# Start of a hybrid decoder step: two column groups in turns, another order of the first transfers, and zero-padded pair matmuls

## The chip, the cores and the metric

The kernel runs on one core of a Trainium2 chip. The metric is the device time of one execution in microseconds (us). Inputs and outputs are float32 and lie in the chip's memory; there is one launch.

## What is computed

One layer of a decoder trunk, for 256 rows of a new sequence (the prompt) and 8 x 4 rows of running sequences (the samples). All 288 rows go through the same weights. Cut to what matters:

```python
proj = x @ w_in                                   # 2048 -> 11280 columns
gB, gC, h, q, k, v, z, b_logit, a_logit, m_a, m_b = split(proj)
conv_out, new_conv_a = causal_depthwise_conv(gC * h, conv_a_buf, conv_a_w)     # width 3
y_a = (gB * conv_out) @ w_a_out
qkv, new_gdn_buf = causal_depthwise_conv(concat(q, k, v), gdn_buf, gdn_conv_w) # width 4
q, k, v = split(silu(qkv)); q, k = l2norm(q), l2norm(k)
o, S = gated_delta_rule(q, k, v, g, beta, S0)     # chunks of 64 rows, 8 heads of 128
y_b = (rms_norm(o) * silu(z)) @ w_b_out
merged = sigmoid(m_a) * y_a + sigmoid(m_b) * y_b
x = layer_norm(ALPHA * x + merged @ w_o)
x = layer_norm(ALPHA * x + relu(x @ w_up)**2 @ w_down)
```

The chunk step of the delta rule is, for each head: `v_new = u - w @ S; o = qd @ S + attn @ v_new; S = S * exp(gl) + kd.T @ v_new`. The convolutions need the last rows of the earlier state (`state_gdn_conv`, `state_conv_a`), here called the history.

## The kernel before, in words

Every large product is cut into **blocks**. A block is a weight tile `raw` of 512 rows (four slices of 128, `KB`) by 256 columns (`GW`), 512 KB. Four blocks that share their 256 columns make a **group** with one accumulator `acc` (two buffers in PSUM); there are 496 blocks. For each block `load` (L164) reads `raw` by a DMA on SyncE's queue, `split_hi` (L173, ScalarE, a cast) and `split_lo` (L179, VectorE, a subtraction) make a rounded high part and the rest, and `matmuls` (L186) issues, for each slice and each half of the columns, three matmuls of 128x128 by 288: hi by xh, hi by xl, lo by xh (L202 to L204). `raw`, `hi` and `lo` have four buffers each. After a group's last block its `evac` functions are called one per following block; they take `acc` out of PSUM and work on. The order of all instructions is written out by hand: the program is one list of blocks, a table `due` of functions to be called ahead of a block, a list `fill` of functions of which one is called behind each triple of matmuls, and generators (`side`) that advance by one step per block.

The activations enter through **`x_tile`** (L732): for each of the 16 slices of 128 features two 128x128 transposes of the prompt and one of the 32 sample rows, on TensorE, then a cast on ScalarE to `xh` and a subtraction on VectorE to `xl`. The columns of x come in four transfers `xr` for the prompt and four of 32 rows for the samples, on SyncE's queue in turns with the first four weight blocks. The 16 transfers of the history (`hwr`, `har`, L723 to L726) are issued on GpSimd's queue from the start on. Eight matmuls on a zero tile (`warm`, L709) come first on TensorE.

The first block's four x tiles come ahead of it; while blocks 0, 1 and 2 run, the twelve others are put between their triples. All three belong to the first group of columns (K, first 256), so block i needs the i-th quarter of x. Weight blocks are split three blocks ahead (`AHEAD`). Constants, layer-norm rows (`lnr`), and the small weight columns `wbar` follow on SyncE's queue (L1286 to L1294). `hist_tiles` (L741) transposes the history and `lnr` at block 4; from there on the convolutions can run. `gates` and then `gdn` (one generator for each half of the heads) are advanced from block 4 on.

In `gdn`, `rep4` (L913) is a copy on GpSimd that lays out the sample keys for a transpose (L917). `aT` holds the masked attention of the 64-row chunks: two heads of a pair lie in partitions 0 to 63 and 64 to 127. For every chunk `p3` (L1188) is the state's update and `p4` (L1192) is `attn @ v_new`, four matmuls with 64 partitions in and 64 out.

Of the kernel before, what the change touches and what calls it, by code (L numbers as in the profile page):

```python
# [9 lines left out]
F32 = mybir.dt.float32  # L10
F32R = mybir.dt.float32r
# [92 lines left out]
def hybrid_kernel(ctx: ExitStack, tc: tile.TileContext, A):  # L104
# [34 lines left out]
    def tt(out, a, b, op):  # L139
        dve.tensor_tensor(out=out, in0=a, in1=b, op=op)  # L140
# [108 lines left out]
    def conv_evac(sec, G, p):  # L249
        def piece(t):  # L250
            hh = 2 * p + t
            ti = sec * 8 + 4 * G + hh
            tl = {}

            def f(ps):
                gpool = gd["pool"]
                w1 = gpool.tile([P, 640], F32, tag="w1", name=nm("w1"), bufs=2)
                pad, cv = w1[:, 0:320], w1[:, 320:640]
                tl["cv"] = cv
                sm = pad[:, 259:315].rearrange("p (b s) -> p b s", s=7)  # L260
                gps.memset(pad[:, 0:3], 0.0)
                gps.tensor_copy(sm[:, :, 0:3], hw[:, ti, 0:24].rearrange("p (b j) -> p b j", j=3))
                act.copy(pad[:, 3:259], ps[:, t, 0:NP_])
                act.copy(sm[:, :, 3:7], ps[:, t, NP_:NT].rearrange("p (b s) -> p b s", s=4))
                c = cv[:, 0:312]
                act.mul(c, pad[:, 0:312], hw[:, ti, 24:25])
                for j in range(1, 4):
                    stt(c, pad[:, j:j + 312], hw[:, ti, 24 + j:25 + j], c, MUL, ADD)
                gps.tensor_copy(stB[:, ti, :].rearrange("p (g j) -> p g j", j=3),
                                pad[:, 256:319].rearrange("p (g s) -> p g s", s=7)[:, :, 0:3])  # L270

            def f2(ps):
# [12 lines left out]
        (a0, a1), (b0, b1) = piece(0), piece(1)  # L285

        def last(ps):
            a1(ps)
            b1(ps)
        return [a0, b0, last]  # L290

    mark = {}
    for G in range(2):
        mark["kqv", G] = len(blocks)
        for sec, c0 in ((1, C_K), (0, C_Q), (2, C_V)):
            for p in range(2):
                add_group(w_in, c0 + 512 * G + GW * p, 0, KT, acts_x, conv_evac(sec, G, p))
        mark["kqv_end", G] = len(blocks)

    def h_evac(p):  # L300
        def f(ps):
# [403 lines left out]
    warm = tx.tile([P, 512], mybir.dt.bfloat16, name="warm")  # L705
    dve.memset(warm, 0.0)
    wps = gtile()
    for _ in range(8):
        pe.matmul(wps, warm[:, 0:P], warm, start=True, stop=True)  # L709
    xr = [tx.tile([P, 3, 512], F32, name=f"xr{i}") for i in range(4)]  # L710
    xpr = A["x_prompt"][0].rearrange("(b p) f -> p b f", p=P)
    xsr = A["x_sample"].rearrange("b t f -> (b t) f")
    sp.dma_start(cf[:, 0:128], A["cf"][:, 0:128])
    for i in range(4):
        c = slice(512 * i, 512 * i + 512)
# [4 lines left out]
    har = tx.tile([76, 256], F32, name="har")  # L720
    for g in range(4):
        c, c2 = slice(768 * g, 768 * g + 768), slice(256 * g, 256 * g + 256)
        gps.dma_start(hwr[28 * g:28 * g + 24, :], A["state_gdn_conv"][0].rearrange("b j c -> (b j) c")[:, c])  # L723
        gps.dma_start(hwr[28 * g + 24:28 * g + 28, :], A["gdn_conv_w"][0][:, c])
        gps.dma_start(har[19 * g:19 * g + 16, :], A["state_conv_a"][0].rearrange("b j c -> (b j) c")[:, c2])
        gps.dma_start(har[19 * g + 16:19 * g + 19, :], A["conv_a_w"][0][:, c2])  # L726
    lnr = tx.tile([33, P], F32, name="lnr")
    gps.memset(epsc[:, 0:1], LN_EPS)
    gps.memset(epsc[:, 1:2], NORM_EPS)
    gps.memset(epsc[:, 2:3], 1.28e-10)  # L730

    def x_tile(k):  # L732
        i, kk = k // 4, k % 4
        g = gtile()
        for b in range(2):
            pe.transpose(g[:, b * P:(b + 1) * P], xr[i][:, b, kk * P:(kk + 1) * P], ident)  # L736
        pe.transpose(g[:, NP_:NT], xr[i][0:NS, 2, kk * P:(kk + 1) * P], ident[0:NS, 0:NS])
        act.copy(xh[:, k, :], g[:, 0:NT])
        tt(xl[:, k, :], g[:, 0:NT], xh[:, k, :], SUB)

    def hist_tiles():  # L741
        g = gtile()
# [114 lines left out]
    def gdn(G):  # L857
# [25 lines left out]
        gps.memset(U128, 0.0)  # L883
        gl = T([P, 4, 2, 64], "gl")
        ss = T([P, 22], "ss")
        red = T([P, 4, 4], "red")
# [23 lines left out]
        pe.transpose(sp2[:, 0:128], kst, ident)  # L910
        pe.transpose(sp2[:, 128:256], qst, ident)

        gps.tensor_copy(wide, four(kst))  # L913
        yield
        ktr = gtile()
        for hh in range(4):
# [246 lines left out]
        for c in range(4):  # L1163
# [24 lines left out]
                pe.matmul(p3[hh % 2][:, hh // 2, :], kdec[r, c, hh // 2, :], v[r, c, hh // 2, :],  # L1188
                          start=True, stop=True)
            for p in range(2):  # L1190
                for par in range(2):
                    pe.matmul(p4[rows[1 - par], p * P:(p + 1) * P], aT[rows[par], 2 * c + p, :], v[rows[par], c, p, :],  # L1192
                              start=True, stop=True)
# [79 lines left out]

    cur = [0]
    aux = []
    his[0] = wp.tile([P, KB, GW], F32R, tag="hi", name=nm("hi"))
    los[0] = wp.tile([P, KB, GW], F32R, tag="lo", name=nm("lo"))
    t = raw.pop(0)
    for k in range(KB + 2):
        if k < KB:  # L1280
            x_tile(k)
        if k > 1:
            act.copy(his[0][:, k - 2], t[:, k - 2])  # L1283
            tt(los[0][:, k - 2], t[:, k - 2], his[0][:, k - 2], SUB)
    load(4)
    sp.dma_start(cf[:, 128:], A["cf"][:, 128:NE])  # L1286
    sp.dma_start(cfe, A["cf"][:, NE:NL])
    sp.dma_start(ci, A["ci"])
    sp.dma_start(lnr[0:16, :], A["ln1_g"].rearrange("o (k p) -> (o k) p", p=P))
    sp.dma_start(lnr[16:32, :], A["ln1_b"].rearrange("o (k p) -> (o k) p", p=P))  # L1290
    sp.dma_start(lnr[32:33, :], A["gdn_norm_w"])
    sp.dma_start(wbar, w_in[:, C_BA:C_BA + 16].rearrange("(k p) c -> p k c", p=P))
    sp.dma_start(arow[:, 0, :], A["a_log"].to_broadcast([P, 8]))
    sp.dma_start(arow[:, 1, :], A["dt_bias"].to_broadcast([P, 8]))  # L1294
    for i in range(3):
        split_hi(i + 1, 2)
        split_lo(i + 1, 2)
        load(i + 5)
        fill.extend(lambda k=k: x_tile(k) for k in range(4 * i + 4, 4 * i + 8))
        matmuls(i)  # L1300
    for i in range(4, AHEAD + 3):
        split_hi(i)
        split_lo(i)
        load(i + 4)
    sgen = side()
    gcm = None
    for p in range(8):
        for n, f in enumerate(residual1(p)):
            at(mark["up"] + 6 + 4 * p + n, f)
    for i in range(3, len(blocks)):  # L1310
        cur[0] = i
        split_hi(i + AHEAD)
        if i == 4:
            hist_tiles()
            tx_cm.__exit__(None, None, None)
            gcm = tc.tile_pool(name="gdn", bufs=1)
# [18 lines left out]
        split_lo(i + AHEAD)  # L1335
        for f in due.pop(i, ()):
            f()
        if i == mark["merge"]:
# [56 lines left out]
```

## Time and profile before

| | us |
|---|---|
| median of 3 runs | 1704.31 |
| lowest and highest | 1704.26, 1704.84 |
| the profiled execution, its own time | 1704.72 |
| its span, first to last instruction | 1702.9 |

The profile is of one execution. Its span leaves out 1.8 us around it; the execution is 0.4 us above the median. In the timeline a row gives start, duration, engine, line, operation, tiles, how many, and in brackets how long the engine sat idle before it and what ended that. PE is TensorE, PEld its weight loads, DVE VectorE, ACT ScalarE, POOL GpSimd, SPq SyncE's DMA queue. Matmuls are pipelined, so the distance of two starts, not the duration, is what one costs.

### The profile page before, as it was taken

The numbers are of one execution on the slowest core, as the hardware profiler recorded it, in microseconds if no ns is written. First come the engines' busy times: TensorE is split into PE (matmuls) and PEld (weight loads), VectorE is DVE, ScalarE is ACT, GpSimd is POOL, SyncE is SP. The second block draws the span as 40 slices with busy tenths as digits, with TensorE's granted clock in tenths as the row PEclk, the third lists the DMA queues.
The fourth block names the chain that finished last, engine by engine and source line by source line (L and its number), as shares of the span: only waits on it lengthen the run. The fifth ranks groups of instructions, "written<-read, shape, count | busy, mean of one in ns | idle before, by whom it ended". The sixth has DMA issues, their size and how long they took to land.

```text
span 1702.9 us, 31111 instructions
## 1 busy us (share of the span) xinstructions
PE 1688.7 (99%) x13077; PEld 1667.2 (98%) x13077; DVE 1013.9 (60%) x1301; ACT 727.6 (43%) x1052; POOL 131.7 (8%) x219
## 2 busy tenths in 40 slices
PE   9999999999999999999999999999999999999997
PEld 7999999999999999999999999999999999999996
DVE  5577885757544444556788744565446554466565
ACT  4675626334543334334445533344334443344331
POOL 2232421023300000000010000000000000000000
PEclk9999999999999999999999999999999999999998
DMA  8464466535655555555565555555555555555552
GB/s 243 141 193 139 122 189 201 149 113 162 183 167 164 171 162 164 170 161 161 166 196 173 168 170 165 162 165 169 162 166 159 170 166 168 162 163 160 173 157 73
DMA packets 272296, 279.69 MB, mean 164 GB/s; under 512 B 12123, under 2 KB 267036, under 8 KB 272024
## 3 DMA queue, kind: packets, MB, share of 16 engines
q1 hardware_dynamic: 267324, 265.80, 51.4%
q0 software_dynamic: 4256, 11.65, 2.5%
q8 instruction: 102, 1.67, 0.4%
q10 hardware_dynamic: 576, 0.26, 0.1%
q14 instruction: 38, 0.30, 0.0%
HBM read 270.19 MB, written 7.48 MB: 163 GB/s over the span
## 4 chain that ended last, share of the span: by engine, by line
PE 99%; DMA 1%; DVE 0%; SPq 0%; issue 0%; ACT 0%
PE acc L202 31%; PE acc L204 31%; PE acc L203 31%; PE g L1021 1%; DMA xr<-in_x_sample_dram 1%; PE g L1009 0%; PE g L1168 0%; PE g L1188 0%; PE g L1192 0%; PE g L1140 0%; PE g L769 0%; PE g L1180 0%; PE g L591 0%; PE g L895 0%; PE g L650 0%; PE g L736 0%
## 5 line engine op out<-in xcount | busy, mean ns | idle before, releaser
L140 DVE TENSOR_TENSOR lo<-raw,hi 128x1024 fp32r<-128x1024 f32 (+2 forms) x502 | 615.7, 1229 | 548.1 <-ACT hi L177 545.5
L177 ACT CAST hi<-raw 128x1024 fp32r<-128x1024 f32 (+1 forms) x498 | 517.8, 1041 | 765.4 <-PE acc L203 711.9
L202 PE MATMUL acc<-xh,hi 128*128 128x288 f32 x1408 | 422.3, 300 | 0.2 <-ACT hi L1283 0.2
L204 PE MATMUL acc<-xh,lo 128*128 128x288 f32 x1408 | 416.4, 296 | 0.0
L203 PE MATMUL acc<-xl,hi 128*128 128x288 f32 x1408 | 416.2, 296 | 0.0
L202 PE MATMUL acc<-dh,hi 128*128 128x290 f32 x1024 | 303.9, 297 | 0.0
L203 PE MATMUL acc<-dl,hi 128*128 128x290 f32 x1024 | 303.2, 296 | 0.0
L204 PE MATMUL acc<-dh,lo 128*128 128x290 f32 x1024 | 302.7, 296 | 0.0
L204 PE MATMUL acc<-hh,lo 128*128 128x288 f32 x1024 | 302.3, 295 | 0.0
L203 PE MATMUL acc<-hl,hi 128*128 128x288 f32 x1024 | 302.3, 295 | 0.0
L202 PE MATMUL acc<-hh,hi 128*128 128x288 f32 x1024 | 302.2, 295 | 0.0
L202 PEld LDWEIGHTS acc<-xh,hi 128*128 128x128 f32 x1408 | 265.2, 188 | 2.8 <-issue 0.7
L203 PEld LDWEIGHTS acc<-xl,hi 128*128 128x128 f32 x1408 | 265.5, 189 | 0.9
L204 PEld LDWEIGHTS acc<-xh,lo 128*128 128x128 f32 x1408 | 265.3, 188 | 0.0
L202 PEld LDWEIGHTS acc<-dh,hi 128*128 128x128 f32 x1024 | 193.6, 189 | 0.1
L204 PEld LDWEIGHTS acc<-dh,lo 128*128 128x128 f32 x1024 | 193.3, 189 | 0.0
L203 PEld LDWEIGHTS acc<-dl,hi 128*128 128x128 f32 x1024 | 193.3, 189 | 0.1
L203 PEld LDWEIGHTS acc<-hl,hi 128*128 128x128 f32 x1024 | 192.5, 188 | 0.0
L204 PEld LDWEIGHTS acc<-hh,lo 128*128 128x128 f32 x1024 | 192.3, 188 | 0.0
L202 PEld LDWEIGHTS acc<-hh,hi 128*128 128x128 f32 x1024 | 192.1, 188 | 0.0
L203 PE MATMUL acc<-ml,hi 128*128 128x288 f32 x256 | 75.6, 295 | 0.0
L204 PE MATMUL acc<-mh,lo 128*128 128x288 f32 x256 | 75.6, 295 | 0.0
(389 smaller groups left out, 1614.3 us busy)
## 6 DMA issues: line engine op xcount, KB each, us to landing
raw<-in_w_in_dram SPq DMA_DIRECT2D x176, 512.0 KB, 3.6
raw<-in_w_up_dram SPq DMA_DIRECT2D x128, 512.0 KB, 3.7
raw<-in_w_down_dram SPq DMA_DIRECT2D x128, 512.0 KB, 3.7
raw<-in_w_o_dram SPq DMA_DIRECT2D x32, 512.0 KB, 3.7
raw<-in_w_a_out_dram SPq DMA_DIRECT2D x16, 512.0 KB, 3.6
raw<-in_w_b_out_dram SPq DMA_DIRECT2D x16, 512.0 KB, 3.6
S<-in_state_gdn_dram POOLq DMA_DIRECT2D x8, 512.0 KB, 7.7
out_dram<-S POOLq DMA_DIRECT2D x8, 512.0 KB, 4.9
```

Of the source, the lines that this page charges most:

```text
L140: dve.tensor_tensor(out=out, in0=a, in1=b, op=op)
L177: act.copy(his[i][:, k:k + step], raw[i][:, k:k + step])
L202: pe.matmul(o, wh, xh_, start=st, stop=False)
L203: pe.matmul(o, wh, xl_, start=False, stop=False)
L204: pe.matmul(o, wl, xh_, start=False, stop=en)
L1021: pe.matmul(out[r, q * 64:q * 64 + 64], a[r, q, :], b[r, q, :], start=True, stop=True)
```

## The change

Five things are changed.

1. The first eight blocks, two groups, are taken in turns: slices 0 to 3 of the first group, slices 0 to 3 of the second, then 4 to 7 of each, and so on. Blocks 2u and 2u+1 need the u-th quarter of x. Both accumulators are in use until block 7. The first group's conv functions for its two halves are called together (`pair`).
2. All sample rows come by one transfer (`xs4`, 128 partitions) on ScalarE's queue and are transposed by four full transposes (`x_sample`). The prompt is transposed four tiles at a time (`x_steps`), and cast and subtracted two slices at a time. The first quarter of the prompt comes in two halves, one on ScalarE's queue. Eleven warm matmuls stand first and four more behind the sample's transposes. The second half of `fill` in blocks 1, 3 and 5 holds the later quarters.
3. The weight splits of the first blocks run two blocks ahead and are issued behind the matmuls of a block. SyncE's queue now has two weight blocks, a quarter of x, two weight blocks, a quarter of x; the constants come one by one behind blocks 2 to 5.
4. The history's 16 transfers wait until `xr[2]` has landed (a one-element copy on GpSimd), and the three of `lnr` follow them on the same queue. `hist_tiles` stands ahead of block 6, `gates` from block 10.
5. In `gdn`, `aT` is 128 wide with zeros, cleared on GpSimd, so that `p4` is two matmuls of 128 by 128 for a chunk; `rep4` is filled by ScalarE.

```diff
+        def pair(ps):
+            a0(ps)
+            b0(ps)
+        if G == 0 and sec == 1 and p == 0:
+            return [pair, last]
...
+    blocks[0:8] = [blocks[4 * (u % 2) + u // 2] for u in range(8)]
...
-    for _ in range(8):
-        pe.matmul(wps, warm[:, 0:P], warm, start=True, stop=True)
-    xr = [tx.tile([P, 3, 512], F32, name=f"xr{i}") for i in range(4)]
+    warm_up(11)
+    xr = [tx.tile([P, 2, 512], F32, name=f"xr{i}") for i in range(4)]
+    xs4 = tx.tile([P, 512], F32, name="xs4")
...
-        sp.dma_start(xr[i][:, 0:2, :], xpr[:, :, c])
-        sp.dma_start(xr[i][0:NS, 2, :], xsr[:, c])
-        load(i)
+    act.dma_start(xr[0][:, :, 256:512], xpr[:, :, 256:512])
+    act.dma_start(xs4, xsr)
+    sp.dma_start(cf[:, 0:128], A["cf"][:, 0:128])
+    sp.dma_start(xr[0][:, :, 0:256], xpr[:, :, 0:256])
+    load(0)
+    load(1)
+    sp.dma_start(xr[1], xpr[:, :, 512:1024])
+    load(2)
+    load(3)
+    sp.dma_start(xr[2], xpr[:, :, 1024:1536])
...
+    gps.tensor_copy(hwr[0:1, 0:1], xr[2][0:1, 0, 0:1])
     for g in range(4):
...
+    gps.dma_start(lnr[0:16, :], A["ln1_g"].rearrange("o (k p) -> (o k) p", p=P))
+    gps.dma_start(lnr[16:32, :], A["ln1_b"].rearrange("o (k p) -> (o k) p", p=P))
+    gps.dma_start(lnr[32:33, :], A["gdn_norm_w"])
...
+    def x_sample():
         g = gtile()
+        for c in range(4):
+            pe.transpose(g[:, c * P:(c + 1) * P], xs4[:, c * P:(c + 1) * P], ident)
...
+        act.copy(xv, gv)
+        tt(xw, gv, xv, SUB)
+
+    def x_steps(i):
+        def prompt(u):
...
+            def turn(k, b):
+                c = (2 * u + k) * P
+                return lambda: pe.transpose(gv[:, k, b * P:(b + 1) * P], xr[i][:, b, c:c + P], ident)
+
+            def out():
+                ks = slice(4 * i + 2 * u, 4 * i + 2 * u + 2)
+                act.copy(xh[:, ks, 0:NP_], gv)
+                tt(xl[:, ks, 0:NP_], gv, xh[:, ks, 0:NP_], SUB)
...
-        aT = T([P, 8, 64], "aT")
+        aT = T([P, 8, P], "aT")
         gps.memset(kqm, 0.0)
-        gps.memset(U128, 0.0)
+        for z in (U128, aT):
+            gps.memset(z, 0.0)
...
-        gps.tensor_copy(wide, four(kst))
+        act.copy(wide, four(kst))
...
-            tt(aT[rows[par]],
+            tt(aT[rows[par], :, 64 - 64 * par:128 - 64 * par],
...
-                for par in range(2):
-                    pe.matmul(p4[rows[1 - par], p * P:(p + 1) * P], aT[rows[par], 2 * c + p, :], v[rows[par], c, p, :],
-                              start=True, stop=True)
+                pe.matmul(p4[:, p * P:(p + 1) * P], aT[:, 2 * c + p, :], v[:, c, p, :], start=True, stop=True)
...
+    for f in x_steps(0):
+        f()
+    x_sample()
+    warm_up(4)
+    split_hi(0, 1)
+    split_lo(0, 1)
...
+    split_hi(1, 2)
+    split_lo(1, 2)
     load(4)
...
+    load(5)
+    sp.dma_start(xr[3], xpr[:, :, 1536:2048])
...
-    for i in range(3, len(blocks)):
+    for i in range(len(blocks)):
         cur[0] = i
-        split_hi(i + AHEAD)
-        if i == 4:
+        if i == 6:
+            split_hi(i + 2)
+            split_lo(i + 2)
+        if i > 5:
+            split_hi(i + AHEAD)
+        if i in (1, 3, 5):
+            a_, b_ = x_steps(i // 2 + 1)
+            idle = lambda: None
+            fill.extend([idle, idle, idle, a_, idle, b_])
+        if i == 6:
             hist_tiles()
...
-        if i > 3 and sgen:
+        if i > 9 and sgen:
...
         matmuls(i)
-        load(i + AHEAD + 4)
+        if i < 6:
+            split_hi(i + 2)
+            split_lo(i + 2)
+            load(i + 6)
+        if i == 6:
+            load(i + 6)
+        if i > 5:
+            load(i + AHEAD + 4)
+        if 2 <= i < 6:
+            rest[i - 2]()
```

More of the change, by code (lines that the diff above doesn't have):

```diff
@@ L707, in hybrid_kernel, with warm_up @@
     wps = gtile()
-    for _ in range(8):
-        pe.matmul(wps, warm[:, 0:P], warm, start=True, stop=True)
-    xr = [tx.tile([P, 3, 512], F32, name=f"xr{i}") for i in range(4)]
-    xpr = A["x_prompt"][0].rearrange("(b p) f -> p b f", p=P)
[L712 to L715, printed above, removed]
-        sp.dma_start(xr[i][:, 0:2, :], xpr[:, :, c])
-        sp.dma_start(xr[i][0:NS, 2, :], xsr[:, c])
-        load(i)
+    def warm_up(n):
+        for _ in range(n):
+            pe.matmul(wps, warm[:, 0:P], warm, start=True, stop=True)
+    warm_up(11)
+    xr = [tx.tile([P, 2, 512], F32, name=f"xr{i}") for i in range(4)]
+    xs4 = tx.tile([P, 512], F32, name="xs4")
+    xpr = A["x_prompt"][0].rearrange("(b p) f -> p b f", p=P)
+    xsr = A["x_sample"].rearrange("b t (j f) -> j (b t) f", j=4)
     hwr = tx.tile([112, 768], F32, name="hwr")
     har = tx.tile([76, 256], F32, name="har")
+    lnr = tx.tile([33, P], F32, name="lnr")
+    act.dma_start(xr[0][:, :, 256:512], xpr[:, :, 256:512])
[8 more added lines that the diff above has]
+    sp.dma_start(xr[2], xpr[:, :, 1024:1536])
+    gps.memset(epsc[:, 0:1], LN_EPS)
+    gps.memset(epsc[:, 1:2], NORM_EPS)
+    gps.memset(epsc[:, 2:3], 1.28e-10)
+    gps.tensor_copy(hwr[0:1, 0:1], xr[2][0:1, 0, 0:1])
     for g in range(4):
@@ L726, in hybrid_kernel, with step, f @@
         gps.dma_start(har[19 * g + 16:19 * g + 19, :], A["conv_a_w"][0][:, c2])
[L727 to L733, printed above, removed]
-        g = gtile()
[L735 to L739, printed above, removed]
+    gps.dma_start(lnr[0:16, :], A["ln1_g"].rearrange("o (k p) -> (o k) p", p=P))
+    gps.dma_start(lnr[16:32, :], A["ln1_b"].rearrange("o (k p) -> (o k) p", p=P))
+    gps.dma_start(lnr[32:33, :], A["gdn_norm_w"])
+    def x_sample():
+        g = gtile()
+        for c in range(4):
+            pe.transpose(g[:, c * P:(c + 1) * P], xs4[:, c * P:(c + 1) * P], ident)
+        gv = g.rearrange("p (c j t) -> p j c t", c=4, j=4)
+        xv, xw = (u.rearrange("p (j c) t -> p j c t", j=4)[:, :, :, NP_:NT] for u in (xh, xl))
+        act.copy(xv, gv)
+        tt(xw, gv, xv, SUB)
+    def x_steps(i):
+        def prompt(u):
+            g = gtile()
+            gv = g.rearrange("p (k t) -> p k t", k=2)
+            steps = []
+            def turn(k, b):
[5 more added lines that the diff above has]
+                tt(xl[:, ks, 0:NP_], gv, xh[:, ks, 0:NP_], SUB)
+            return [turn(k, b) for k in range(2) for b in range(2)], out
+        def step(part):
+            def f():
+                turns, out = part()
+                for g in turns:
+                    g()
+                out()
+            return f
+        return [step(lambda: prompt(0)), step(lambda: prompt(1))]
     def hist_tiles():
@@ L1275, in hybrid_kernel @@
     aux = []
[L1276 to L1284, printed above, removed]
-    load(4)
[L1286 to L1304, printed above, removed]
+    for f in x_steps(0):
[4 more added lines that the diff above has]
+    split_lo(0, 1)
+    rest = [lambda: sp.dma_start(cf[:, 128:], A["cf"][:, 128:NE]),
+            lambda: sp.dma_start(cfe, A["cf"][:, NE:NL]),
+            lambda: sp.dma_start(wbar, w_in[:, C_BA:C_BA + 16].rearrange("(k p) c -> p k c", p=P)),
+            lambda: (sp.dma_start(ci, A["ci"]),
+                     sp.dma_start(arow[:, 0, :], A["a_log"].to_broadcast([P, 8])),
+                     sp.dma_start(arow[:, 1, :], A["dt_bias"].to_broadcast([P, 8])))]
+    split_hi(1, 2)
+    split_lo(1, 2)
+    load(4)
+    load(5)
+    sp.dma_start(xr[3], xpr[:, :, 1536:2048])
     sgen = side()
@@ L1334, in hybrid_kernel @@
                 gd["ao"] = ap_.tile([P, 2, H, NT], F32, tag="ao", name="ao")
-        split_lo(i + AHEAD)
+        if i > 5:
+            split_lo(i + AHEAD)
         for f in due.pop(i, ()):
@@ L1360, in hybrid_kernel @@
         matmuls(i)
-        load(i + AHEAD + 4)
+        if i < 6:
[4 more added lines that the diff above has]
+            load(i + 6)
+        if i > 5:
+            load(i + AHEAD + 4)
+        if 2 <= i < 6:
+            rest[i - 2]()
     for i in sorted(due):
```

## The prediction, made before the changed kernel was run

> **What bounds the kernel now.** I read the page first (busy times, then the chain that ended last), then the start of TensorE's timeline, where most of the change lies, then the queues that feed it.
>
> ```profile
> span 1702.9 us, 31111 instructions
> PE 1688.7 (99%) x13077; PEld 1667.2 (98%) x13077; DVE 1013.9 (60%) x1301; ACT 727.6 (43%) x1052; POOL 131.7 (8%) x219
> PE 99%; DMA 1%; DVE 0%; SPq 0%; issue 0%; ACT 0%
> ```
>
> TensorE is the bound from end to end: a gain needs work taken off TensorE, or its slow start shortened. Busy is not busy at full speed, so the start's rows come next.
>
> ```profile
> 1.19 3.60 PE L709 MATMUL g<-warm 128*128 128x512 bf16 x8 [1.19 <-DVE warm L706]
> 9.57 0.61 PE L202 MATMUL acc<-xh,hi 128*128 128x288 f32 x1 [0.21 <-ACT hi L1283]
> 18.35 0.44 PE L202 MATMUL acc<-xh,hi 128*128 128x288 f32 x1
> 18.59 0.44 PE L203 MATMUL acc<-xl,hi 128*128 128x288 f32 x1
> 23.27 0.30 PE L203 MATMUL acc<-xl,hi 128*128 128x288 f32 x1
> 23.40 0.29 PE L204 MATMUL acc<-xh,lo 128*128 128x288 f32 x1
> 24.26 0.30 PE L203 MATMUL acc<-xl,hi 128*128 128x288 f32 x1
> 31.25 0.30 PE L202 MATMUL acc<-xh,hi 128*128 128x288 f32 x1
> 34.44 0.55 PE L744 MATMUL g<-cf,hwr 112*128 112x112 f32 x4
> 35.43 0.40 PE L202 MATMUL acc<-xh,hi 128*128 128x288 f32 x1
> ```
>
> Product matmuls start 0.24 apart at 18.35 and 0.13 apart at 23.27: at 18.35 TensorE still runs at about half speed, and the eight warm matmuls had not cured it. Block 3 starts at 31.25 and takes 34.44 - 31.25 = 3.19; the history's transposes take 35.43 - 34.44 = 0.99. An x tile stands between the matmuls of 23.40 and 24.26; without it they would be 2 x 0.13 apart, so it costs 0.60. At 31.25, then, three blocks (9.6) and 16 x tiles (9.6) are done, and 12 us went to waiting and half speed.
>
> **Part 1: the start.** Four full transposes in the tail show the price of a batch of the new kind, and two views show how fast data arrives:
>
> ```profile
> 1612.07 0.30 PE L204 MATMUL acc<-hh,lo 128*128 128x288 f32 x1
> 1612.20 0.60 PE L591 MATMUL g<-cf,acc 128*128 128x128 f32 x4
> 1612.56 0.38 PE L202 MATMUL acc<-hh,hi 128*128 128x288 f32 x1
> 1612.77 0.29 PE L203 MATMUL acc<-hl,hi 128*128 128x288 f32 x1
> ```
>
> ```profile
> 0.00:10.00 10.00, 7.50 (x22) 3.33 (x22) 2.09 (x6) 3.37 (x7) 6.46 (x16) 1.00 0.78 212
> 10.00:20.00 10.00, 9.15 (x35) 7.15 (x35) 5.27 (x12) 4.41 (x11) 2.19 (x7) 1.00 1.09 299
> ```
>
> ```profile
> 9.12 0.40 ACT L1283 CAST hi<-raw 128x256 fp32r<-128x256 f32 x1 [0.17 <-DMA raw<-in_w_in_dram]
> 18.27 1.14 ACT L177 CAST hi<-raw 128x512 fp32r<-128x512 f32 x2 [0.30 <-DMA raw<-in_w_in_dram]
> ```
>
> The batch costs (1612.77 - 1612.07) - 0.26 = 0.44. The last two columns of the windows are the DMA engines' share and GB/s. The bytes moved are 2.12 MB by 10 us and 0.30 MB per us after that; the queues are full (share 1.09). Block 0's weights had landed at 9.12, when about 1.9 MB had moved, and block 2's at 18.27, after 4.6 MB; counting all that was issued ahead of them (constants, x, weights, history), 1.4 and 3.8 MB. So a transfer lands when its own running sum plus 0.5 to 0.8 MB has moved. The new order's sums (x quarter, weight block: 0.52 MB each, samples 0.26, first constants 0.07) are 1.4 MB for block 0's weights, 1.9, 2.4 for the second x quarter, 2.9 for block 2, 3.5, and 4.0 for the third quarter. Their landings come out at 9.0, 11, 13, 14.7, 16.5 and 18.3.
>
> The first product matmul thus starts where it does now: I take 9.7, since ScalarE must cast a sample batch first. From there block 0 needs 3.2 plus 0.3 for its first low part (13.2). Block 1 needs 3.2 and two batches, 4.1 in all (17.3). Block 2's weights land at 14.7, and cast, subtraction and one x subtraction follow: 1.05, 1.23 (below) and an estimated 0.65 by width give 17.6. Blocks 2 to 5 take 3.2 + 4.1 + 3.2 + 4.1, up to 32.2, with every transfer there at least 2 us early. Then six blocks and all of x are done, against three at 31.25: 3 x 3.19 - 0.95 = **8.6 gained**. Later rows stay as they are, since TensorE has no idle time there that the order of groups could change.
>
> This assumes full speed from 9.7. Eleven warm matmuls last 11 x 0.45 = 5 us from 1.19, and four more stand behind the samples. If the speed comes only at 12.8, 3.1 us at half cost 1.5, of which 0.4 hides in block 2's wait: 1.1. The rule that bears on it is in the Trainium skill, "TensorE: Matmul & The Clock Gate", Part 1: full clock follows one busy window of 3.4 us that runs freely, and Part 4 adds that transposes hardly count as busy. By that rule the new warm-up holds a whole window in about 4 of 10 phases, and the sum would lose up to 1.1 in the others. The trace agrees in that 3.60 us of warm matmuls left half speed behind; no row fixes the phase.
>
> **Part 2: the history's wait.** It is moved behind the third x quarter and three transfers longer, and TensorE, which works in order, meets it at block 6. Queued behind it there are all blocks from 6 on.
>
> ```profile
> 1.29 0.70 POOL L723 DMA_DIRECT2D hwr<-in_state_gdn_conv_dram  x1 [0.84 <-POOLq L1382]
> 6.27 0.52 POOL L723 DMA_DIRECT2D hwr<-in_state_gdn_conv_dram  x1 [0.75 <-DMA hwr<-in_state_gdn_conv_dram]
> 12.48 0.51 POOL L726 DMA_DIRECT2D har<-in_conv_a_w_dram  x1
> ```
>
> ```profile
> DMA to landing us min/median/max: 4.5/6.4/7.2
> ```
>
> ```profile
> DMA to landing us min/median/max: 1.8/3.2/4.7
> ```
>
> The first landing row is that of `hwr` at the start, with full queues; the second is that of the state's output (L1262), later. Eight transfers go out 0.51 apart, and the ninth waits for the first one's landing (6.27). So 19 transfers are two such rounds and three more: with landings of L, the last one lands 3L + 1.5 after the first issue, or 9.7 + L where L is under 4.1. Now sixteen are issued in 11.7 us; three more and a landing make it 19.5. At the short end it is 9.7 + 3.2 = 12.9. From 18.3 the history is there at 31.2 to 37.8. The weight queue is full early in that stretch and emptier at its end, so I take the middle, 34.6: TensorE waits **2.4** at 32.2. Bounds: nothing to 5.6.
>
> A long wait can also cost speed:
>
> ```profile
> 1680.00:1686.00 6.00, 5.45 (x42) 5.22 (x40) 0.96 (x4) 0.00 (x0) 0.00 (x0) 1.00 0.00 0
> 1686.00:1690.00 4.00, 1.44 (x7) 0.61 (x7) 3.77 (x14) 0.68 (x3) 0.00 (x0) 0.85 0.00 0
> 1690.00:1694.00 4.00, 3.30 (x9) 1.90 (x8) 3.78 (x12) 0.52 (x2) 0.00 (x0) 0.50 0.42 157
> ```
>
> The granted clock (third column from the end) falls to half some 3 us after the last dense matmuls. Getting it back took from about 12.4 to 19.7 at the start, 3.6 us lost; with dense matmuls I take 2.5. It applies to waits above 3.4 only.
>
> **Part 3: the chunks.**
>
> ```profile
> 192.69 0.65 PE L1192 MATMUL g<-v,aT 64*64 64x128 f32 x8
> 193.28 0.49 PE L1102 MATMUL g<-b 128*128 128x128 f32 x2
> 193.52 0.38 PE L202 MATMUL acc<-xh,hi 128*128 128x288 f32 x1
> 205.18 0.60 PE L1180 MATMUL g<-v,U 128*128 128x128 f32 x4
> 205.62 0.39 PE L1120 MATMUL g<-b 128*128 128x128 f32 x2
> 205.76 0.38 PE L202 MATMUL acc<-xh,hi 128*128 128x288 f32 x1
> ```
>
> The quarter-size matmuls take 193.28 - 192.69 = 0.59 per chunk; two full ones (L1180) take 0.44. Behind the small tiles the next pair takes 0.24, behind full ones 0.14: up to 0.10 for the switch, which may only move to p3. So 0.15 to 0.25 for each of 8 chunks, 1.2 to 2.0; I take **1.6**. A rule speaks against it: the Trainium skill, "TensorE: Matmul & The Clock Gate", Part 3, has small tiles in different rows and columns run together, and then the pairs would cost what the full ones do, and the sum would be 1.6 smaller. The trace disagrees by half: 0.074 apiece against 0.11 for full ones, not 0.055.
>
> **Edits at nothing.** The moved copy and the larger clear have cover:
>
> ```profile
> L913 POOL COPY vmh<-kqs x2: 942/1012/1081, 102.0 to 286.0; 128x512 f32<-128x512 f32 x2
> L883 POOL MEMSET U<- x2: 955/974/993, 90.2 to 265.2; 128x1024 f32 x2
> ACT hi L177 <- PE acc L203: 155.5, 79, 4.4
> L177 ACT CAST hi<-raw 128x1024 fp32r<-128x1024 f32 (+1 forms) x498 | 517.8, 1041 | 765.4 <-PE acc L203 711.9
> L140 DVE TENSOR_TENSOR lo<-raw,hi 128x1024 fp32r<-128x1024 f32 (+2 forms) x502 | 615.7, 1229 | 548.1 <-ACT hi L177 545.5
> ```
>
> ScalarE waits 79 times between 60 and 500 us for a free buffer of hi, so 0.6 more there is hidden; without that cover it costs 1.2 in all. The second clear adds 1 us to GpSimd, which is 8% busy. At block 7 the first group's evacuation must free its accumulator within 3.19: one cast (1.05) and some 1.7 of copies and scaling fit, if block 10's weights are there. With both accumulators held, a late one costs up to 1; I take nothing. The gates start six blocks later but end one block later.
>
> **The sum.** 8.6 - 2.4 + 1.6 = 7.8 off the profiled execution's 1704.7, hence off the median of 1704.3 too: **1696.5**.
>
> **Rivals.**
> - History in time: nothing waits at block 6, 10.2 gained: 1694.1; with a start half a microsecond earlier and the upper chunk price 1693. For it: fewer weights are in flight by then. Against: full queues at 18 us. 0.17.
> - History late by 5.6 with the clock lost: 10.2 - 5.6 - 2.5 = 2.1, 1702.2. For it: the first landing row. 0.18.
> - Slower: the same wait, at block 6. It eats the whole gain when it passes 7.7 us, that is when landings average 6.7; at 7.8 the result is 3.4 slower, 1707.7. Against: the longest landing shown is 7.2. 0.05.
> - The warm-up doesn't do what it says, or the chunks give nothing: 1697.6 and 1698.1. 0.10.
>
> **How the numbers follow.** The forecast has 0.50. About 0.2% (3.4 us) can be told from no change, so faster means under 1700.9. The forecast, the first and the last rival lie there, and a small part of the second with a shorter wait: 0.82. Same takes most of the second, 0.12; slower is 0.06. The range runs from 1693 to 1702, which takes in both bounds of the wait.
>
> **What would show it.** Right: 0.13 spacing from the first product matmuls on, block 6 near 32, an idle row of 1 to 4 us at the history's transposes with a GpSimd transfer as its releaser, p4 in four passes of 0.11. Wrong: idle time between blocks 1 to 5 (weights later than my sums), 0.24 spacing beyond 13 us, a wait for the accumulator at block 8, or an idle row at the history above 6 us.

## The result, and the profile after

The changed kernel is slower: 1710.11 us (median of 6 runs, 1709.41 to 1711.23) against 1704.57 of the kernel before beside it, a ratio of 1.0034 with a 95% interval of 1.0024 to 1.0044. The forecast of 1696.5 was wrong in its sign. The profiled execution took 1709.7 us. Its page, with the busy times and the chain that ended last:

```profile
span 1707.8 us, 31019 instructions
PE 1684.7 (99%) x13040; PEld 1667.2 (98%) x13040; DVE 1012.4 (59%) x1292; ACT 727.0 (43%) x1045; POOL 123.5 (7%) x223
PE 90%; DVE 2%; ACT 1%; issue 1%; POOL 0%; ACTq 0%; DVEq 0%
```

The share of TensorE is 99% as before, but it is idle for 1707.8 - 1684.7 = 23.1 us, against 14.2 before, and the chain now runs through VectorE and ScalarE for some per cent. TensorE's waits name two places that the kernel before does not have (total, times, longest, in us):

```profile
PE g L965 <- ACT vmh L961: 6.0, 1, 6.0
PE g L757 <- DMA xs<-in_x_sample_dram: 3.8, 1, 3.8
```

The start, and the place of the long wait, in TensorE's timeline:

```profile
11.26 1.11 PE L757 MATMUL g<-cf,xs 128*128 128x128 f32 x4 [3.77 <-DMA xs<-in_x_sample_dram]
13.52 0.80 PE L202 MATMUL acc<-xh,hi 128*128 128x288 f32 x1
16.76 0.44 PE L202 MATMUL acc<-xh,hi 128*128 128x288 f32 x1
17.41 0.29 PE L202 MATMUL acc<-xh,hi 128*128 128x288 f32 x1
37.16 0.55 PE L791 MATMUL g<-cf,hwr 112*128 112x112 f32 x4
38.14 0.40 PE L202 MATMUL acc<-xh,hi 128*128 128x288 f32 x1
110.02 1.12 PE L965 MATMUL g<-cf,vmh 128*128 128x128 f32 x4 [6.01 <-ACT vmh L961]
110.79 0.59 PE L202 MATMUL acc<-xh,hi 128*128 128x288 f32 x1
115.00 0.29 PE L202 MATMUL acc<-xh,hi 128*128 128x288 f32 x1
```

The first product matmul comes at 13.52 (9.57 before), because the samples land late, and half speed (durations of 0.44 and more) lasts to about 17.2. The warm matmuls had brought full speed: the granted clock is 0.91 over 8 to 11 us; the 3.77 us of waiting for the samples lost it again (0.50 from 11 to 17.2). The history's transposes at 37.16 show no wait. Block 6 starts at 38.14, in the kernel before at 41.91:

```profile
41.91 0.29 PE L202 MATMUL acc<-xh,hi 128*128 128x288 f32 x1
```

So the start did gain, 3.8 us. At 104.0 TensorE then stands for 6.01 us ahead of the transposes of `rep4`. These take 110.79 - 110.02 = 0.77 instead of 0.36 (rows of the kernel before, below), and block 24 behind them 115.00 - 110.79 = 4.21 instead of 3.19, both at half speed at first.

What the wait is for is read from the two engines behind it. ScalarE, then GpSimd, both of the changed kernel:

```profile
90.07 1.28 ACT L866 ACT_TABLE_LOAD   x1
95.04 0.56 ACT L266 ACTIVATE w<-w,hw 128x312 f32<-128x312 f32 x1 [1.89 <-POOL w L262]
101.76 0.56 ACT L266 ACTIVATE w<-w,hw 128x312 f32<-128x312 f32 x1 [2.37 <-POOL w L262]
105.63 1.28 ACT L276 ACT_TABLE_LOAD   x1
109.35 0.62 ACT L961 COPY vmh<-kqs 128x512 f32<-128x512 f32 x1
```

```profile
92.05 0.22 POOL L879 COPY gpt<-qt 64x48 f32<-64x48 f32 x1 [7.60 <-ACT qt L870]
95.09 3.59 POOL L911 DMA_DIRECT2D S<-in_state_gdn_dram  x4
98.67 1.08 POOL L929 MEMSET b<- 128x1152 f32 x1
99.67 0.98 POOL L931 MEMSET U<- 128x1024 f32 x1
100.57 0.97 POOL L931 MEMSET aT<- 128x1024 f32 x1
101.50 0.22 POOL L262 COPY w<-hw 128x24 f32<-128x24 f32 x1
```

The copy `rep4` (L961) comes at 109.35, at the end of a queue on ScalarE that was held up twice by GpSimd, at the convolution's evacuation (L266 needs GpSimd's L262). GpSimd in turn was busy first with the gate copies (`gpt`, `gsw`), which had themselves waited 7.60 for ScalarE, then with the set-up of `gdn`: the state's four loads and three clears, 95.09 to 101.5. In the kernel before the same set-up lay where nobody waited, and the copy was early:

```profile
85.62 3.60 POOL L864 DMA_DIRECT2D S<-in_state_gdn_dram  x4
90.20 0.99 POOL L883 MEMSET U<- 128x1024 f32 x1
101.97 0.94 POOL L913 COPY vmh<-kqs 128x512 f32<-128x512 f32 x1
104.33 0.60 PE L917 MATMUL g<-cf,vmh 128*128 128x128 f32 x4
104.69 0.38 PE L202 MATMUL acc<-xh,hi 128*128 128x288 f32 x1
```

So by block 111 of 496 the changed kernel is 4.6 behind: +3.8 from the start and +1.1 from the chunks (priced below), -6.0 for the wait, -1.4 for the half speed behind it (0.4 at the transposes, 1.0 in block 24), -0.9 for four short waits at blocks 47 to 94 that the kernel before does not have either. That is -3.4; the other 1.2 is spread over rows that I have not named.

### The profile page after: what moved, and what is told of

Same layout as the page of the kernel before. It is cut to its first block, busy times and chain, and to the rows that moved or that the text cites. A ratio compares the mean times of both kernels' runs of the same rounds, so it can differ in the third digit from the quotient of the medians.

```text
span 1707.8 us, 31019 instructions
## 1 busy us (share of the span) xinstructions
PE 1684.7 (99%) x13040; PEld 1667.2 (98%) x13040; DVE 1012.4 (59%) x1292; ACT 727.0 (43%) x1045; POOL 123.5 (7%) x223
## 4 chain that ended last, share of the span: by engine, by line
PE 90%; DVE 2%; ACT 1%; issue 1%; POOL 0%; ACTq 0%; DVEq 0%
PE acc L202 29%; PE acc L203 29%; PE acc L204 29%; PE g L1069 1%; DVE lo L140 1%; DVE w L143 1%; PE g L1057 0%; PE g L1236 0%; PE g L1239 0%; PE g L1188 0%; PE g L1216 0%; PE g L598 0%; PE g L657 0%; DVE v L143 0%; ACT hi L177 0%
## 5 line engine op out<-in xcount | busy, mean ns | idle before, releaser
L140 DVE TENSOR_TENSOR lo<-raw,hi 128x1024 fp32r<-128x1024 f32 (+1 forms) x500 | 613.2, 1230 | 541.6 <-ACT hi L177 539.4
```

## The experiments

Three candidates stood for the 6 us: the copy's place on ScalarE (A), the later gates and all that hangs on them (B), the extra clear (C). A fourth theory (D) concerned the samples' landing.

**The copy on GpSimd again.**

```diff
-        act.copy(wide, four(kst))
+        gps.tensor_copy(wide, four(kst))
```

> The changed kernel with one edit undone: the copy rep4 is on GpSimd again. In the changed kernel (1710.1) TensorE waits 6.01 us for this copy at 104.0, and runs some 3 us at half speed behind it, about 7.4 us in all. Theory A (the copy's place on ScalarE costs it, since it stands there behind late casts): GpSimd is idle from 101.9 on, so the copy is done by about 103, TensorE does not wait, and the time is 1702.5 to 1704. Theory B (ScalarE as a whole is late, because GpSimd's gate copies, state loads and clears come six blocks later and hold up the convolutions' evacuation): the wait moves to the next thing that comes from ScalarE, at least 3 us of it stay, 1706 or more.

Measured: 1708.47, ratio 1.0018 (1.0008 to 1.0027). B's forecast is met, A's is not. TensorE's wait:

```profile
PE g L965 <- POOL vmh L961: 3.4, 1, 3.4
```

and the copy in GpSimd's timeline:

```profile
108.33 1.54 POOL L961 COPY vmh<-kqs 128x512 f32<-128x512 f32 x1 [3.92 <-DVE red L948]
```

The wait is 2.6 shorter, so A explains less than half of it. I had overlooked a reader: `rep4` shares its buffer with the squares that VectorE reduces (L948), and these come from ScalarE, so the copy is late on any engine when ScalarE is late. This profile had a wait of 1.6 at block 6 besides, for `lnr`, so the profiled execution gained almost nothing.

**The gates from block 7.**

```diff
-        if i > 9 and sgen:
+        if i > 6 and sgen:
```

> The changed kernel with the gates started at block 7 rather than 10; the copy rep4 stays on ScalarE, the clear of aT on GpSimd. Theory B: GpSimd's four pairs of gate copies come near 82 rather than at 92, so the state loads (3.59) and the clears (3.0) lie ahead of the evacuation that ScalarE begins at 98.9, ScalarE's two waits for GpSimd (1.89 and 2.37) go, the copy comes some 4 to 5 us earlier, TensorE waits under 1.5 us, and the time is 1703 to 1705. Theory A: the copy still stands behind ScalarE's casts, the wait stays at 4 us or more, and the time is 1708 or more.

Measured: 1700.91, ratio 0.9979 (0.997 to 0.9989), 9.2 below the changed kernel, and faster than before. B is confirmed, with 2 us more than its 1703 to 1705. Of ScalarE's two waits for GpSimd the one of 2.37 is gone; one of 1.89 stays behind the gate copies, but it now ends at 84.3 and not at 95.0, far ahead of the copy `rep4`. The set-up now runs 84.36 to 90.7, ahead of the evacuation of 92.4, and the copy still on ScalarE costs TensorE little:

```profile
84.36 3.59 POOL L911 DMA_DIRECT2D S<-in_state_gdn_dram  x4
100.46 0.66 PE L965 MATMUL g<-cf,vmh 128*128 128x128 f32 x4 [0.69 <-ACT vmh L961]
```

**The chunks as they were.** `aT` 64 wide, not cleared, `p4` in eight small matmuls.

> The changed kernel with the chunk outputs p4 as they were: aT 64 wide, no clear of it, eight quarter-size matmuls per chunk. Theory C (the clear of aT, 0.97 us on GpSimd ahead of the evacuation's copy, makes the wait): the wait falls by as much as the clear took, to 5.0 us, or goes altogether if a turn of the queue hangs on it; the chunks cost 8 x 0.2 = 1.6 more; 1710.7, or 1704.5 if it goes. Theory A and B: the wait stays between 5 and 6 us, and the difference to the changed kernel is the price of the chunks less one microsecond: 1710 to 1711. If the padded pairs gain nothing, 1709.

Measured: 1709.65, ratio 1.0031 (1.0019 to 1.0043). The wait is 5.1 instead of 6.0: the clear is worth about what it lasts (0.97) and no more. C falls as the main cause. The time is 0.4 below what A and B gave (1710 to 1711), which the interval (3.2 to 7.3 us above the kernel before) can't tell from it.

**The samples on SyncE's queue.**

```diff
-    act.dma_start(xs4, xsr)
     sp.dma_start(xr[0][:, :, 0:256], xpr[:, :, 0:256])
+    sp.dma_start(xs4, xsr)
```

> The changed kernel with the one DMA of the samples moved from ScalarE's queue to SyncE's, behind the first quarter of x and ahead of block 0's weights. In the changed kernel the samples are there at 11.26 only, though issued at 1.25, and the first product matmul starts at 13.52. Theory D (ScalarE's queue gets a small share of the transfers beside SyncE's full one, and that is what makes the start late): the samples land after 0.85 MB, at 6 to 7 us, the first product matmul starts at 9.7 to 10.5, and 3 to 3.8 us are gained: 1706.3 to 1707.1. Rival (the transfers as a whole are the limit, whatever their queue): the weights of block 0 come 0.26 MB later, the first product matmul at 11.5 or later, and the time is 1708 to 1710. If half speed then lasts as long after the first product matmul as now (3.7 us), the gain is the same; if it ends at the same time (17.2), half of it goes.

Measured: 1709.36, ratio 1.0029 (1.0019 to 1.0039). D is right on the start and wrong on the total:

```profile
8.65 0.66 PE L757 MATMUL g<-cf,xs 128*128 128x128 f32 x4 [1.70 <-DMA xs<-in_x_sample_dram]
10.35 0.40 PE L202 MATMUL acc<-xh,hi 128*128 128x288 f32 x1 [0.17 <-ACT hi L177]
35.99 0.22 PE L796 MATMUL g<-cf,lnr 33*128 33x33 f32 x1 [2.48 <-DMA lnr<-in_gdn_norm_w_dram]
```

```profile
38.00:40.00 2.00, 2.00 (x10) 2.00 (x10) 0.00 (x0) 0.00 (x0) 0.00 (x0) 0.50 0.87 184
```

Block 0 starts 3.2 earlier and at full speed, block 5, for that, 4.5 earlier. At block 6 stands the wait that the prediction had put there, 2.48 long (forecast 2.4). By its row it is for `lnr`, whose three transfers the change put behind the history's on the same queue; the history's own transposes, just ahead of it, show no wait. Behind it the granted clock is 0.50 (in the row of the windows, third column from the end) and block 6 takes 4.82 instead of 3.29. So 4.0 of the 4.5 are given back at once.

**The later gates alone, in the kernel before** (`i > 3` becomes `i > 9`).

> The kernel before with one edit of the change alone: the gates start at block 10 instead of 4. Everything else, the start and the copy on GpSimd too, stays as before (1704.6). Theory B (the later gates alone push GpSimd's gate copies, state loads and clears onto the evacuation, and ScalarE with them): TensorE waits 2.4 to 3.4 us at the transposes of rep4 (3.36 in the run with the copy on GpSimd, less up to one for the clear that is not there) and loses 1 to 1.5 behind it: 1708 to 1709.5. Rival E (the later gates hurt only together with the faster start, which leaves ScalarE and GpSimd less time up to there): the wait is under 1 us, 1704 to 1705.5.

Measured: 1709.37, ratio 1.0029 (1.0018 to 1.004). This one edit makes the kernel before as slow as the whole change did. The waits of TensorE and of ScalarE:

```profile
PE g L917 <- POOL vmh L913: 2.5, 1, 2.5
ACT w L266 <- POOL w L262: 3.4, 2, 1.9
```

B again; rival E, that it needs the faster start, falls.

**Padded pairs alone, and the copy on ScalarE alone, in the kernel before.**

> The kernel before with the zero-padded pairs alone (aT 128 wide and cleared as a whole, p4 in four passes). In the run with the gates from block 7 each of the 8 chunks came out 0.15 us shorter against the kernel before. If that is the edit's price: 1.2 less than before, 1703.3 (the prediction's 1.6 would give 1702.9; pairs that cost what the small tiles do, 1704.5). If the clear of aT ahead of the evacuation's copy made a wait there of its own, as theory C had it, TensorE would show a wait of about 1 us at the transposes of rep4 and the time would be 1704.5.

> The kernel before with the copy rep4 on ScalarE alone, the gates where they were. The prediction held it hidden in ScalarE's waits (nothing lost, 1704.5). Theory A in what is left of it: it stands behind a cast and four small copies there, as in the run with the gates from block 7, and TensorE waits 0.3 to 0.8 us for it at the first group's transposes: 1704.8 to 1705.3.

Measured: 1703.10 with the pairs, ratio 0.9991 (0.9982 to 1.0), and 1704.43 with the copy, ratio 0.9998 (0.9989 to 1.0007). A chunk in the first:

```profile
192.44 0.71 PE L1192 MATMUL g<-v,aT 128*128 128x128 f32 x4
192.99 0.39 PE L1103 MATMUL g<-b 128*128 128x128 f32 x2
193.13 0.38 PE L202 MATMUL acc<-xh,hi 128*128 128x288 f32 x1
```

The four passes take 0.55 (the small ones 0.59), the pair behind them 0.14 (0.24): 0.14 per chunk, and each chunk brings the blocks behind it forward by that much, 1.1 for all eight. The medians differ by 1.6, with an interval of 0 to 3.1. In the second, TensorE does not wait at `rep4` at all. Where the gates come early, both edits are as harmless as the prediction had them.

**Where in the queues the later gates hurt.** Six runs separate the parts. First the eight gate copies (`gpt`, `gsw`) moved from GpSimd to VectorE:

> The changed kernel with the gates as late as there, and their eight copies (gpt, gsw) on VectorE instead of GpSimd. In the changed kernel GpSimd stands idle for 7.60 us until 92.05 for these copies' operand, with the state loads (3.59) and the clears (3.0) queued behind them, and ScalarE's evacuations then wait 1.89 and 2.37 for GpSimd. Theory G (it is GpSimd's order that does it): the loads and clears are done by 91, ScalarE's two waits go, the copy rep4 comes 4.3 us earlier, TensorE waits 1.7 us or less at its transposes and keeps its clock or loses up to 1: 1702.5 to 1705. Rival S (ScalarE is late of itself, by its table loads of 1.28 us for the gates and back between 85 and 107): the wait stays at 3 us or more, 1706.5 or more.

Measured: 1710.56, ratio 1.0036 (1.0022 to 1.005), a wait of 6.3, which is what rival S gave (3 us or more, 1706.5 or more). Theory G falls as I had put it: GpSimd still met the evacuation's last copy, which waits for ScalarE, and did the set-up from 94.87 to 101.2, ahead of the next evacuation; ScalarE waited 3.3 for it in one piece.

Then the first group's steps moved against the evacuations. These come one per block behind a group, at blocks 20 and 21, then 24 and 25. The set-up stands between those of 20 and 21 in the changed kernel, ahead of both with the gates from block 9 (`i > 8`), behind both in the other run (`mark["kqv", G] + 20` becomes `+ 22` for the first half of the heads):

> The changed kernel with the gates from block 9 instead of 10, so that the first group's set-up (state loads, clears) stands one block earlier, at block 20 as in the kernel before. Theory H (the set-up's 6.6 us on GpSimd must lie in the long pause between two groups' evacuations; it hurts where it stands ahead of an evacuation that ScalarE already wants): behind the gate copies it would start near 89 and end near 96, and the evacuation of about 92 waits for it some 4 us, so most of the loss stays: 1707 to 1711. Rival L (each block of lateness costs, wherever it lies): a third of the way to the run with block 7, 1706 to 1707, with a wait of 3 to 4 us.

> The changed kernel with the gates as late as there, and the first group's set-up two blocks later still (from block 22 on), behind both evacuations of the group that ends at block 19. Theory H: GpSimd's 6.6 us then lie between 97 and 104, ahead of the next group's evacuation at about 107; ScalarE's wait of 2.37 goes and the copy rep4 comes early enough: TensorE waits under 1.5 us, 1702 to 1704.5, though the set-up is later. Rival L: later is worse, TensorE waits 6 us or more, 1710 or more.

Measured: 1709.36, ratio 1.0029 (1.0018 to 1.0039), with a wait of 6.4; and 1708.61, ratio 1.0023 (1.0014 to 1.0033), with a wait of 1.7 there. ScalarE's longest wait for GpSimd in the first, and TensorE's at a chunk in the second:

```profile
ACT w L266 <- POOL w L262: 4.8, 1, 4.8
```

```profile
PE g L1236 <- DVE v L140: 2.0, 1, 2.0
```

One block earlier doesn't help, since the set-up then holds up the evacuation ahead of which it stands, for 4.8. Behind the evacuations it holds up nobody, and the wait falls to 1.7 (H: under 1.5). But the time missed its forecast by 4: the steps that are now two blocks late wait later, 2.0, 1.2 and 0.9 at the chunks.

Last, only GpSimd's set-up was taken out and issued at block 15, between two groups; then the gate copies went to VectorE as well:

> The changed kernel with the gates and the first group's steps exactly as late as there; only the set-up's GpSimd work (four state loads, three clears, 6.6 us) is taken out of the first step and issued at block 15, between two groups' evacuations. Theory H (that work stands ahead of an evacuation that ScalarE already wants): ScalarE's wait of 2.37 goes, the one of 1.89 behind the gate copies stays, TensorE's wait at rep4's transposes falls from 6.0 to about 3.6, and 2.4 to 4 us are gained: 1706 to 1708. Rival L (the steps of the group are late as such, on TensorE and ScalarE): wait of 5 us or more, 1709 or more.

> As the run before it, and the eight gate copies on VectorE. Theory H: now both of ScalarE's waits for GpSimd are gone (4.3 us in all), TensorE's wait falls to 1.7 us, and the clock behind it is lost for 1 us or not at all: 1703.5 to 1705.5. Rival S (ScalarE's own table loads, 1.28 us each): more than 3 us of wait stay, 1706.5 or more.

Measured: 1707.92, ratio 1.002 (1.001 to 1.003), and 1706.41, ratio 1.0011 (1.0002 to 1.002). TensorE's waits at `rep4`'s transposes, which are L960 there, in the one and the other:

```profile
PE g L960 <- ACT vmh L956: 3.7, 1, 3.7
```

```profile
PE g L960 <- ACT vmh L956: 3.1, 1, 3.1
```

ScalarE's only pause from 88 to 107 in the second is this one:

```profile
93.96 0.21 ACT L890 ACTIVATE sx<-s 128x4 f32<-128x4 f32 x1 [1.65 <-DVE s L887]
```

The set-up's place makes 2.3 of the 6.0 (2.4 expected). With no wait of ScalarE for GpSimd left, 3.1 stay, so rival S is right for part of it. Not for all: the pause of 1.65 was 0.48 in the changed kernel, and VectorE, which it waits for, has the gate copies now, so up to 1.2 of the 3.1 can be this edit's own doing. The rest is ScalarE's own work. The windows of 60 to 85 us show why (ACT is the fourth busy time), before, changed, and changed with the gates from block 7:

```profile
60.00:85.00 25.00, 25.00 (x193) 25.00 (x192) 15.78 (x32) 20.32 (x45) 8.21 (x20) 1.00 0.50 148
```

```profile
60.00:85.00 25.00, 25.00 (x190) 24.04 (x189) 11.05 (x24) 14.48 (x30) 3.61 (x8) 1.00 0.34 107
```

```profile
60.00:85.00 25.00, 25.00 (x192) 24.80 (x191) 14.11 (x30) 19.69 (x44) 6.19 (x19) 1.00 0.40 117
```

Five to six microseconds of ScalarE's work were pushed out of a stretch with room into the one with the evacuations; between 79 and 107 it does six table loads of 1.28 in the changed kernel, two with the gates from block 7, none in the kernel before. A last run kept the gates at block 7 and only the group's steps a block late:

> The changed kernel with the gates from block 7 (1700.9 so far) but the first group's steps from block 21 as in the changed kernel, so that the set-up stands between the two evacuations again while ScalarE's gate work with its table loads is long over. Theory S+H (of the 6.0 us wait, the late gate work on ScalarE is worth 3.1 and GpSimd's place 2.3): GpSimd, free of gate copies, does the 6.6 us from about 85 to 92 or, behind the first evacuation's copy, from about 93 to 100, where the second evacuation waits some 2 us; TensorE waits 0 to 2.5 us at rep4's transposes, and the later steps lose the 0.9 us at blocks 47 to 94 as in the changed kernel: 1701.5 to 1704.5. If the steps' lateness by a block were the cause whatever ScalarE does (rival L), the wait stays at 5 us or more: 1707 or more.

Measured: 1705.57, ratio 1.0004 (0.9994 to 1.0013), with a wait of 2.1 as expected, and 1 us above the upper forecast. ScalarE's and TensorE's waits:

```profile
ACT w L266 <- POOL w L262: 4.7, 2, 2.8
PE g L965 <- ACT vmh L961: 2.1, 1, 2.1
```

So of the 9.2 us between 1700.9 and 1710.1, 4.7 come from the group's steps being one block late, 4.5 from the gates' own work being three blocks late. That the greater part of these 4.5 is ScalarE's share of the gates is argued, not shown: the copies on GpSimd were moved by themselves (nothing gained, then 1.5), ScalarE's work never was.

**The versions that the experiments point to.** Gates from block 7 and samples on SyncE's queue; then with the history's loads waiting for the second quarter of x (`xr[1]`); then with the copy on GpSimd too.

> The changed kernel with two edits: the gates from block 7, and the samples' DMA on SyncE's queue. With the gates alone it is 1700.9; the samples' move brought block 4 forward by 10.05 - 6.57 = 3.5 us against that run. Theory F (the faster start runs into the history's wait): the wait at block 6 takes 2.5 and the half speed behind it 1.5, as in the run with the samples alone, and nothing is gained: 1700.5 to 1702. Rival (that wait was a chance of that run, since it was 0 to 1.6 in the others): under 1 us of wait, 1697 to 1698.5.

> As the run before it, and the history's loads wait for the second quarter of x instead of the third, so that they start some 4 us earlier. Theory F: the history is there before TensorE meets it, no wait and no half speed at block 6, the whole start counts: 1696.7 to 1698. Rival (the history's 0.42 MB, now among the weights of blocks 2 to 5, make these late by up to 1.4 us, and TensorE waits there in place of block 6): 1698.5 to 1700.5.

> As the run before it, and the copy rep4 on GpSimd again. With the gates from block 7 TensorE still waited 0.69 us for this copy on ScalarE. Theory A in what is left of it (its place on ScalarE costs these 0.7): the wait goes, 0.5 to 0.9 less than the run before it, about 1696.5. Theory B alone: the copy then waits on GpSimd for VectorE's reduction and takes 0.9 to 1.5 us in place of 0.62, nothing is gained, within 0.3 us of the run before it.

Measured: 1699.96, ratio 0.9973 (0.9962 to 0.9985); 1696.37, ratio 0.9954 (0.9942 to 0.9967); 1696.48, ratio 0.9951 (0.9939 to 0.9964). All three lie within 0.6 of their forecasts. Theory F holds: in the first, 2.5 of wait at block 6 and 1.5 of half speed; in the second, neither:

```profile
32.15 0.55 PE L791 MATMUL g<-cf,hwr 112*128 112x112 f32 x4
33.13 0.40 PE L202 MATMUL acc<-xh,hi 128*128 128x288 f32 x1
```

The copy's engine makes no difference that can be told. The second version beats both kernels by 8.1 and 13.7 us.

## Why the prediction was wrong, point by point

- **The step that failed** stands under "Edits at nothing": "The gates start six blocks later but end one block later." I priced that at zero, and had read it wrongly besides: the gates take eleven steps, one per block, so they end six blocks later too (block 20 instead of 14); what comes one block later is the group's steps behind them (block 21 instead of 20). The gates moved 6 us of ScalarE's work, and the one block put GpSimd's 6.6 us between two evacuations. By the runs it is worth 9.2 us in the changed kernel (gates from block 10 against block 7), and alone makes the kernel before 4.9 slower (1709.4). I had named the queues and read their busy shares (GpSimd 8% busy, ScalarE with 79 pauses between 60 and 500 us), but not what lies ahead of the moved work in each queue, nor who waits there.
- **"Hidden" copy and clear:** right in their own setting (no wait at `rep4` in the kernel before), wrong in the changed one, where the cover was gone: of the wait of 6.0, 2.6 are the copy's place and 0.9 the clear. The text's own clause, "without that cover it costs 1.2 in all", was too small, since it counted the copy and not the queue ahead of it.
- **Part 1, the start:** the sum of the blocks was right and its first term wrong. Blocks 1 to 5 took 4.06, 3.19, 4.06, 3.19 and, with the history, 5.04, nearly as forecast; the first product matmul came at 13.52 instead of 9.7, since the samples landed at 11.26, where the running sum, which counts all queues as one, had them ahead of block 0's weights, by 9.0; and 3.7 us of half speed followed, priced at 1.1 among the rivals. With the samples on SyncE's queue and the history early, the history's transposes start at 32.15; the forecast was 32.2.
- **Part 2, the history's wait:** absent in the profile of the changed kernel, whose start was 4 us late (1.5 to 1.7 in three other profiles with that start); 2.48 where the start was nearly as forecast. There both ends came later than forecast, TensorE at 33.5 for 32.2 and the last rows at 36.0 for 34.6, so that the 2.4 is met in part by luck. The clause that half speed threatens only after waits "above 3.4" fell: waits of 1.6 and 2.5 there cost 1.5 each, one of 1.7 none.
- **Part 3, the chunks:** 1.1 for a forecast of 1.6, a little under the lower bound of 1.2. In three of the eight chunks all of the 0.10 for the switch of tile size was gained, but the four full ones took 0.55 instead of 0.44; in the other five they took 0.47, and the matmul behind them gained 0.02. Why they differ stays open: the small tiles of p3 stand ahead of them in all eight. By the rule in the Trainium skill, "TensorE: Matmul & The Clock Gate", Part 3, nothing would have been gained; the trace goes against it here.
- **The total** of 1696.5 is what the version with the mended order gives (1696.4), partly by chance: its start gained 8.8 by block 6, its chunks 1.1, and some 2 were lost elsewhere.

## What to carry to other kernels

When a change shifts a stream of side work by even one step, list for each in-order queue what stands ahead of it and behind it after the shift, and who waits there; a low busy share says nothing on that. GpSimd is the queue to look at first, because issuing four DMAs and clearing three buffers occupied it here for 6.6 us, and an evacuation that needs one tiny copy from it passes its delay on to ScalarE and TensorE. A faster start is worth only as much as the next transfer that it runs into allows, so move that transfer too.

## What the runs showed of the hardware

- **A transfer on a second queue can come very late.** The samples were issued second on ScalarE's queue, at 1.25, and landed at 11.26; issued third on SyncE's, TensorE had them at 8.65 and, in the second version above, at 8.05. Counting the trace's DMA packets by queue, from 6 to 9 us ScalarE's queue got 20 to 23 a microsecond (2 KB each) and SyncE's 147 to 213. It is not the queue as such: from 2 to 4 us, when ScalarE's queue carried its half quarter of x in rows of 1 KB, it got 275 packets and SyncE's 250. The Trainium skill, "DMA: Bandwidth & Descriptors", "Queues, rings and completion order", states that each DMA engine goes round between queues and drains a packet of about 9 to 17 descriptors before it switches; the ratio of 7 to 10 is of that kind, if the trace counts descriptors and a row of the samples is a packet by itself. No run tests that. The same page's "Issuing engines are not separate DMA queues" says that another issuing engine saves only issue time; here it cost up to 3 us of landing time.
- **Half speed comes back after short waits.** 1.58 us of wait at block 6 cost 1.5 us of half speed in one profile (the copy on GpSimd again), 1.74 cost none in another (set-up at block 15 and copies on VectorE), 2.48 cost 1.5. At the transposes of `rep4`, 2.1 of wait in the last of the six runs left a granted clock of 0.64 from 105 to 109, while 2.5 in the kernel before with later gates left it at 1.00 from 100 to 112. In the changed kernel the clock is 0.67 over the wait itself, 104 to 110; at 1.00 and then 0.50 that puts the fall, by estimate, 2.0 us after TensorE stopped. The Trainium skill, "TensorE: Matmul & The Clock Gate", Part 1, puts the fall behind an idle window of about 3.4 us whose phase runs freely; with the 1.0 us of small transposes around the waits at block 6 the phase may explain the scatter there, but even with them the gap of 1.58 that lost speed came to 2.6, shorter than the window. That was not tried by itself.
